# The beginning of the first attention layer: q and k projected step by step with the loading of the stream, their weights in halves on a second queue, the gate's projection last

## The chip, the cores and the metric

The kernel runs on one core of one Trainium2 chip. The metric is the device time of one execution in microseconds, as a median over runs. A profiled execution of the same program gives the trace: when each instruction ran on TensorE (PE, with its weight loads PEld), VectorE (DVE), ScalarE (ACT), GpSimd (POOL) and SyncE (SP), and what the DMA queues moved.

## The reference, cut to what matters

The program is a decoder trunk of two layers over 512 tokens of width 1024. The first layer is forgetting attention (FoX); the second, its MLPs and the latent attention are not touched by the change. What the changed part must compute:

```python
def fox_mixer(h, w_in, b_f, w_out):          # h = rms_norm(x, g)
    proj = h @ w_in                           # q, k, v: 1024 columns each; gate: 16
    q, k, v = ...                             # 16 heads of 64
    f_logit = proj[..., 3 * FOX_WIDTH:] + b_f
    cum = jnp.cumsum(jax.nn.log_sigmoid(f_logit), axis=1)
    # logits of a head: q.k * scale + cum[query] - cum[key], causal
    ctx = softmax(logits) @ v
    return ctx.reshape(B, S, FOX_WIDTH) @ w_out
```

## The kernel before, in words

Everything is float32 in two parts: a value is cast to a high part (ScalarE, `nc.scalar.copy`) and the difference is kept as a low part (VectorE). A product is then three matmuls, high by high, high by low and low by high (`three`, called by `linear`). The stream lies feature-major: eight tiles `xs[k]` of 128 features by 512 tokens. `scaled` multiplies a tile by the norm's gain and splits it into `h[k]`; the norm's factor per token (`rstd`) is applied later, to the results. Weights come in pieces, whose order stands in `pieces()` (L74) and, for the array in memory, in `_pack` (L1231). `piece(name)` takes the next one, and `emit_piece` (L202) loads it on SP's queue into one of two `raw` buffers and splits it into one of three `whi` and three `wlo` buffers, one piece ahead.

The FoX part begins at L433. SP is given x's eight tiles, with the gate's piece (16 columns of 8 steps, 64 KB) after the first and the first q piece (512 KB) after the fourth. Then come, as the program is written: `h`; the gate's projection into a bank `fps`, its weights spread into tiles of 128 columns a step that are cleared first, 24 matmuls; the squares of x and their sum; q's projection for the first pair of heads (24 matmuls); `rstd_of` (L276: eight small matmuls, then a reciprocal root on VectorE and GpSimd); k's (24); `rstd_tile` (L313: spread over 128 partitions by TensorE, copied by ScalarE); and v's first 512 columns in four pieces of 24 matmuls into four banks. After the first of these the program has `qk_parts` (L457), which scales and splits q and k, and `forget_sums` (L485): the gate's logits by rstd, bias, log-sigmoid, a cumulative sum of nine doubling steps on VectorE, and a store to `csc` in device memory. `start` (L540) loads a pair's two rows of it, broadcast over 128 partitions, into `nb`, and the softmax of each step subtracts that.

Attention runs in steps, one pair of heads and one block of 128 queries at a time, with two score banks. Between steps a `Filler` puts later matmuls: the next pairs' q and k projections, more of v, the output projection. Twelve are put ahead of the first step (L606), and 12 after each step.

No order is written by hand in this part. The instructions are ordered when the program is built, by the order in the text and by when each is expected to be ready, and each engine then works its own list in order. The engines' calls go through a wrapper, so nearly all rows of the trace carry its line, L111; they are told apart by their tiles (`acc`, `sc` and `tp` are the banks of this part, `r` the split tiles, `t` the plain ones).

Of the kernel before, what the change touches and what calls it, by code (L numbers as in the profile page):

```python
# [11 lines left out]
F32 = mybir.dt.float32  # L12
# [5 lines left out]
P = 128  # L18
D = 1024
S = 512  # L20
# [52 lines left out]

def pieces():  # L74

    out = [("f", 128)]
    out += [("qk", 1024)] * 2 + [("v", 1024)] * 4
    for p in range(1, FH // 2):
        out += [("v4", 1024)] * (2 * V4_BEFORE.count(p)) + [("qk", 1024)] * 2
    out += [("fo", 1024)] * 8  # L80
    out += [("ffn0", 1024)] * 40
    out += [("ka", 1024)] * 6
    out += [("kvb_v", 1024), ("kvb_n", 1024)] + [("qb_r", 384), ("qb_n", 768)] * 2
    out += [("kvb_n", 1024), ("qb_r", 384), ("qb_n", 768), ("kvb_v", 1024), ("qb_r", 384), ("qb_n", 768)]
    out += [("mo", 1024)] * 8
    out += [("ffn1", 1024)] * 32
    return out
# [9 lines left out]
def trunk(ctx: ExitStack, tc: tile.TileContext, xT, wts, gains, fing, rope, out):  # L97
# [53 lines left out]
    def nm(s):  # L151
        uid[0] += 1
        return f"{s}{uid[0]}"
# [7 lines left out]
    def tt(shape=(P, S)):  # L161
        return tp_.tile(list(shape), F32, tag="t", name=nm("t"))

    def f32(ap):
        return ap.bitcast(F32)
# [36 lines left out]
    def emit_piece(n):  # L202
        name, w = PIECES[n]
        raw = wpool.tile([P, 1024], F32, tag="raw", name=nm("raw"), bufs=2)
        nc.sync.dma_start(raw[:, :w], wts[OFFS[n] : OFFS[n] + P * w].rearrange("(p w) -> p w", p=P))
        if n in APART:

            his, los = [rt(), rt()], [rt(), rt()]
            for j in range(2):
                split(raw[:, j * S : (j + 1) * S], his[j], los[j])  # L210
            state["ready"][n] = [(his[k // 4][:, c], los[k // 4][:, c]) for k in range(KD) for c in [slice(k % 4 * P, k % 4 * P + P)]]
            return
        hi = wpool.tile([P, 1024], F32R, tag="whi", name=nm("whi"))
        lo = wpool.tile([P, 1024], F32R, tag="wlo", name=nm("wlo"))
        if name == "f":
            hv, lv = (t.rearrange("p (k c) -> p k c", c=P) for t in (hi, lo))
            rv = raw[:, :w].rearrange("p (k c) -> p k c", c=FH)
            nc.vector.memset(f32(hi), 0.0)
            nc.vector.memset(f32(lo), 0.0)
            nc.scalar.copy(hv[:, :, :FH], rv)  # L220
            nc.vector.tensor_tensor(lv[:, :, :FH], rv, f32(hv[:, :, :FH]), op=ALU.subtract)
        else:
            nc.scalar.copy(hi[:, :w], raw[:, :w])
            nc.vector.tensor_tensor(lo[:, :w], raw[:, :w], f32(hi[:, :w]), op=ALU.subtract)
        state["ready"][n] = (hi, lo)
# [35 lines left out]
    def scaled(x, gname, k):  # L261
        hi, lo = rt(), rt()
        nc.scalar.activation(out=hi, in_=x, func=AF.Copy, scale=g(gname, k))
        nc.vector.scalar_tensor_tensor(out=lo, in0=x, scalar=g(gname, k), in1=f32(hi), op0=ALU.mult, op1=ALU.subtract)
        return hi, lo
# [162 lines left out]
    with ExitStack() as fx:  # L428
        vpool = fx.enter_context(tc.tile_pool(name="fox_v", bufs=12))
        apool = fx.enter_context(tc.tile_pool(name="fox_a", bufs=2))  # L430
        dpool = fx.enter_context(tc.tile_pool(name="fox_d", bufs=1, space=bass.MemoryType.DRAM))

        xs = [tt() for _ in range(KD)]  # L433
        for k in range(KD):
            nc.sync.dma_start(xs[k], xT[:, k, :])
            if k == 0:
                emit_piece(0)
            if k == 3:
                emit_piece(1)
        h = [scaled(xs[k], "mix0", k) for k in range(KD)]  # L440


        fps = bank("acc")
        linear(fps, piece("f"), h)
        acc = xs[0]
        for k in range(KD):
            square_sum(acc, xs[k], k == 0, xs[k])
        qk = {}
        qk_ps = []
        for _ in range(2):  # L450
            qk_ps.append(bank("acc"))
            linear(qk_ps[-1], piece("qk"), h)
            if len(qk_ps) == 1:
                r = rstd_of(acc, D)
        rstd = rstd_tile(r)

        def qk_parts(pp, scale):  # L457
            t = tt()
# [25 lines left out]

        def forget_sums():  # L485

            z, e = tt(), tt()
            z, e = z[:FH], e[:FH]
            nc.vector.tensor_tensor(z, fps[:FH], rstd[:FH], op=ALU.mult)
            nc.vector.tensor_scalar_add(z, z, gsb[:FH, GCOL["bf"][0] : GCOL["bf"][0] + 1])  # L490
            nc.scalar.activation(out=e, in_=z, func=AF.Abs)
            nc.scalar.activation(out=e, in_=e, func=AF.Exp, scale=-1.0)
            nc.vector.tensor_scalar_add(e, e, 1.0)
            nc.scalar.activation(out=e, in_=e, func=AF.Ln)
            cur = tt()[:FH]
            nc.vector.scalar_tensor_tensor(out=cur, in0=z, scalar=0.0, in1=e, op0=ALU.min, op1=ALU.subtract)
            nc.vector.tensor_scalar_mul(cur, cur, -1.0)
            d = 1
            while d < S:
                nxt = tt()[:FH]  # L500
                nc.vector.tensor_copy(nxt[:, :d], cur[:, :d])
                nc.vector.tensor_tensor(nxt[:, d:], cur[:, d:], cur[:, : S - d], op=ALU.add)
                cur, d = nxt, 2 * d
            csc = dpool.tile([FH, S], F32, name="csc")
            nc.sync.dma_start(csc, cur)
            return csc

        accs = [bank(t) for t in ("sc", "sc", "tp", "tp")]
        for kp in range(4):
            whi, wlo = piece("v")  # L510
            for tb in range(NB):
                for k2 in range(2):
                    k = kp * 2 + k2
                    c = slice(k2 * S, (k2 + 1) * S)
                    t = slice(tb * P, (tb + 1) * P)
                    three(accs[tb], whi[:, c], wlo[:, c], h[k][0][:, t], h[k][1][:, t], k == 0, k == KD - 1, flip=True)
            if kp == 0:
                qk[0] = [qk_parts(pp, scale) for pp, scale in zip(qk_ps, QK_SCALES)]
                csc = forget_sums()
        for tb in range(NB):  # L520
# [710 lines left out]
def _pack(i):  # L1231
    W = FH * FHD
    parts = []
    fw = i["fox_w_in"][0]
    parts.append(_cols(fw, 3 * W, FH))
    parts += [_cols(fw, 0, P), _cols(fw, W, P)]
    b = _cols(fw, 2 * W, S)
    parts += [b[:, 2 * kp : 2 * kp + 2] for kp in range(4)]
    for p in range(1, 8):
        for q in range(2):  # L1240
            if V4_BEFORE[q] == p:
                b = _cols(fw, 2 * W + (q + 2) * 256, 256)
                parts += [b[:, :4], b[:, 4:]]
        parts += [_cols(fw, p * P, P), _cols(fw, W + p * P, P)]
    parts += [_cols(i["fox_w_out"][0], f * P, P) for f in range(8)]

    def up(layer):
        return [_cols(i["ffn_w_up"][layer], f * P, P) for f in range(DFF // P)]

    def down(layer):  # L1250

        w = i["ffn_w_down"][layer].reshape(DFF // HALF, 2, 2, P, 2, S)
        return [w[hf, :, a, :, b].transpose(1, 0, 2) for hf in range(DFF // HALF) for a in range(2) for b in range(2)]

    parts += up(0)
    parts += [_cols(i["ffn_w_down"][0][CHUNKS * D :], f * P, P) for f in range(8)]
    ka = i["mla_w_kv_a"]
    r = _cols(ka, KVR, ROPE)
    six = [_cols(ka, 0, P), _cols(ka, P, P), np.concatenate([r, r], axis=2)]
    six += [_cols(i["mla_w_q_a"][0], b * P, P) for b in range(3)]  # L1260
    for part in range(2):
        ks = list(range(4 * part, 4 * part + 4))
        parts += [np.concatenate([six[2 * n][:, ks], six[2 * n + 1][:, ks]], axis=1) for n in range(3)]
    kb = i["mla_w_kv_b"].reshape(KVR, MH, 2, NOPE)
    v = kb[:, :, 1].reshape(KVR, MH * NOPE)
    qb = i["mla_w_q_b"][0].reshape(QR, MH, NOPE + ROPE)
    vs = [_cols(v, half * S, S) for half in range(2)]
    ns = [np.concatenate([_blk(kb[:, h, 0], slice(None)) for h in range(4 * half, 4 * half + 4)], axis=1) for half in range(2)]
    qs = []
    for p in range(4):  # L1270
        qs.append(_blk(qb[:, 2 * p : 2 * p + 2, NOPE:].reshape(QR, 2 * ROPE), slice(None)))
        qs.append(np.concatenate([_blk(qb[:, 2 * p + e, :NOPE], slice(None)) for e in range(2)], axis=1))
    parts += [vs[0], ns[0]] + qs[:4] + [ns[1]] + qs[4:6] + [vs[1]] + qs[6:]
    parts += [_cols(i["mla_w_out"][0], f * P, P) for f in range(8)]
    parts += up(1)
    assert [x.size // P for x in parts] == [w for _, w in PIECES]
    parts += down(0)[: 2 * CHUNKS * 4] + down(1)
    return np.concatenate([np.ascontiguousarray(x).reshape(-1) for x in parts])
# [46 lines left out]
```

## Time and profile before

| | us |
|---|---|
| median of 3 runs | 1151.25 |
| lowest, highest | 1150.25, 1151.32 |
| the profiled execution's own time | 1152.35 |
| its span, first to last instruction | 1150.6 |

A profile is read from the engine that is busy for most of the span, and then from what ended its idle times. A row of the timeline gives the start in us, the duration in us, the engine, the line, the operation, the tile written and the tiles read, shapes and count; in brackets stands the idle time before it and what ended that. Where matmuls follow each other their rows overlap, because the duration includes the way through the array; their pace is read from their starts or from a chain's row divided by its count. A row of the chain of waits gives start, us, engine, tile and count.

### The profile page before, as it was taken

What the parts mean: (1) busy time and instruction counts of PE and PEld (TensorE: products, weight loads), DVE (VectorE), ACT (ScalarE), POOL (GpSimd) and SP (SyncE); (2) the same over time, 40 slices, a digit from 0 to 9 for tenths busy, and PEclk for the clock granted to TensorE, in tenths of its full rate; (3) what the DMA queues carried; (4) which work ended last, traced back from release to release, by engine and by line L of the source; (5) the groups of instructions that cost most, each with busy time, mean ns of one, the idle gap of its engine ahead of it and who ended that gap; (6) DMA issues with size and microseconds to landing.
All of it is one profiled execution on the core that took longest, in us unless ns stands there. A gap on an engine that the chain in (4) does not pass through costs nothing.

```text
span 1150.6 us, 14300 instructions
## 1 busy us (share of the span) xinstructions
PE 1122.5 (98%) x5356; PEld 916.1 (80%) x5356; DVE 783.1 (68%) x1413; ACT 574.6 (50%) x1053; POOL 24.0 (2%) x86
## 2 busy tenths in 40 slices
PE   8999999999999999999999899999999999999996
PEld 5777887787888888888887768788788888888875
DVE  6797888763457676677793688836356675765775
ACT  5555655553554454444352566635555544445611
POOL 1000000001000000000001100000100000000000
PEclk9999999999999999999999899999999999999998
DMA  5332222152815215212343121312531521611301
GB/s 186 130 102 81 75 82 84 37 165 85 317 37 167 90 55 183 74 56 65 119 159 105 34 65 51 110 55 92 187 143 58 185 68 56 201 56 37 128 1 74
DMA packets 36566, 116.66 MB, mean 101 GB/s; under 512 B 4224, under 2 KB 4864, under 8 KB 36496
## 3 DMA queue, kind: packets, MB, share of 16 engines
q1 hardware_dynamic: 35888, 114.15, 30.3%
q8 instruction: 42, 0.69, 0.2%
q0 software_dynamic: 320, 1.05, 0.2%
q10 hardware_dynamic: 288, 0.55, 0.1%
q14 instruction: 28, 0.23, 0.1%
HBM read 109.40 MB, written 6.32 MB: 101 GB/s over the span
## 4 chain that ended last, share of the span: by engine, by line
PE 92%; DVE 3%; DMA 2%; issue 1%; ACT 1%; POOL 1%; SPq 0%; POOLq 0%; ACTq 0%; DVEq 0%
PE up L111 33%; PE acc L111 20%; PE go L111 18%; PE sc L111 8%; PE tp L111 7%; PE keep L111 6%; DVE r L111 1%; DMA raw<-wts 1%; DVE wlo L111 1%; DVE t L111 1%; ACT r L111 1%; DMA t<-xT 0%; DMA nb<-csc 0%; DVE sl L111 0%; DVE rs L111 0%
## 5 line engine op out<-in xcount | busy, mean ns | idle before, releaser
L111 PE MATMUL acc<-r,whi 128*128 128x512 f32 x600 | 194.4, 404 | 5.0 <-ACT whi L111 5.0
L111 PE MATMUL up<-r,r 128*128 128x512 f32 x808 | 193.3, 391 | 2.5 <-DVE r L111 1.4
L111 PEld LDWEIGHTS up<-r,r 128*128 128x128 f32 x808 | 151.0, 188 | 34.9 <-DVE r L111 2.3
L111 PE MATMUL up<-r,whi 128*128 128x512 f32 x544 | 170.8, 390 | 0.8 <-ACT s L111 0.8
L111 DVE TENSOR_TENSOR t<-s,t 128x512 fp32r<-128x512 f32 x84 | 57.9, 689 | 127.5 <-ACT t L111 127.4
L111 DVE TENSOR_TENSOR wlo<-raw,whi 128x1024 fp32r<-128x1024 f32 (+3 forms) x95 | 111.3, 1171 | 39.4 <-ACT whi L111 38.8
L111 ACT CAST whi<-raw 128x1024 fp32r<-128x1024 f32 (+3 forms) x95 | 95.5, 1008 | 84.0 <-PE acc L111 33.5
L111 PEld LDWEIGHTS acc<-r,whi 128*128 128x128 f32 x600 | 109.6, 190 | 31.1 <-ACT whi L111 5.1
L111 ACT ACTIVATE s<-up 128x512 f32<-128x512 f32 x56 | 33.5, 597 | 190.8 <-PE up L111 190.8
L111 PEld LDWEIGHTS up<-r,whi 128*128 128x128 f32 x544 | 101.7, 188 | 22.4 <-ACT s L111 1.5
L111 PE MATMUL acc<-r,wlo 128*128 128x512 f32 x300 | 118.3, 394 | 0.1
L111 PE MATMUL up<-r,wlo 128*128 128x512 f32 x288 | 112.1, 389 | 0.0
L111 PE MATMUL go<-r,t 128*128 128x512 f32 x360 | 86.5, 389 | 0.0
L111 PE MATMUL sc<-r,r 128*128 128x512 f32 (+6 forms) x480 | 80.5, 356 | 1.6 <-ACT r L111 1.4
L111 PE MATMUL go<-whi,t 128*128 128x512 f32 x240 | 78.7, 389 | 0.0
L111 PEld LDWEIGHTS go<-r,t 128*128 128x128 f32 x360 | 67.6, 188 | 14.0
L111 PEld LDWEIGHTS sc<-r,r 64*128 64x128 f32 (+1 forms) x480 | 55.4, 186 | 25.0 <-issue 9.0
L111 ACT ACTIVATE t<-t,sm 128x512 f32<-128x512 f32 (+3 forms) x96 | 53.4, 558 | 34.7 <-DVE sm L111 34.2
L111 PEld LDWEIGHTS acc<-r,wlo 128*128 128x128 f32 x300 | 56.7, 189 | 12.9 <-DVE wlo L111 0.4
L111 DVE TENSOR_TENSOR r<-raw,r 128x512 fp32r<-128x512 f32 x72 | 46.5, 685 | 26.6 <-ACT r L111 26.6
L111 PEld LDWEIGHTS up<-r,wlo 128*128 128x128 f32 x288 | 54.1, 188 | 11.3
L111 DVE TENSOR_TENSOR r<-q,r 128x512 fp32r<-128x512 f32 x94 | 60.4, 684 | 0.0
(180 smaller groups left out, 1868.1 us busy)
## 6 DMA issues: line engine op xcount, KB each, us to landing
raw<-wts SPq DMA_DIRECT2D x122, 512.0 KB, 3.5
q<-wts SPq DMA_DIRECT2D x56, 512.0 KB, 4.6
nb<-csc SPq DMA_DIRECT2D x8, 512.0 KB, 4.7
t<-xT SPq DMA_DIRECT2D x8, 256.0 KB, 6.2
r<-xT SPq DMA_DIRECT2D x8, 256.0 KB, 6.0
xmid<-r SPq DMA_DIRECT2D x8, 256.0 KB, 6.9
r<-xmid SPq DMA_DIRECT2D x8, 256.0 KB, 4.2
xkeep<-r SPq DMA_DIRECT2D x8, 256.0 KB, 2.3
```

What stands on the lines that cost most here:

```text
L111: ins = fn(*args, **kw)
```

## The change

It touches the beginning of the FoX part, the gate's tiles and the order of the pieces.

- q's and k's first pieces come first in memory, then the gate, then v.
- Their `raw`, `whi` and `wlo` tiles are taken directly. Four loads, the halves of 512 columns (4 of the 8 contraction steps) of q and of k, are issued from ScalarE's queue; SP's queue has only x's eight tiles, back to back.
- One loop over the eight steps k: at k = 0 and k = 2 the halves are split, q's ahead of `scaled` and k's behind it (those of k = 2 serve steps 4 to 7); then three matmuls of that step for q and three for k, into two banks.
- The gate follows, through `piece("f")`. Its weights lie in one tile of 64 columns a step: high part in columns 0 to 15, low part in 32 to 47, zero between. Per step one matmul with 64 columns meets the high part of `h`, and one with the first 32 columns meets the low part: 16 matmuls. The two halves of the result (partitions 0 to 15 and 32 to 47) are added in `forget_sums`, by a copy on ScalarE across partitions and an addition on VectorE.
- Then the squares of x and `rstd_of`; `rstd_tile` comes after the first v piece.

```diff
 def pieces():
-    out = [("f", 128)]
-    out += [("qk", 1024)] * 2 + [("v", 1024)] * 4
+    out = [("qk", 1024)] * 2 + [("f", 128)] + [("v", 1024)] * 4
...
         hi = wpool.tile([P, 1024], F32R, tag="whi", name=nm("whi"))
-        lo = wpool.tile([P, 1024], F32R, tag="wlo", name=nm("wlo"))
+        lo = None if name == "f" else wpool.tile([P, 1024], F32R, tag="wlo", name=nm("wlo"))
         if name == "f":
-            hv, lv = (t.rearrange("p (k c) -> p k c", c=P) for t in (hi, lo))
+            hv = hi[:, : KD * 64].rearrange("p (k c) -> p k c", c=64)
             rv = raw[:, :w].rearrange("p (k c) -> p k c", c=FH)
-            nc.vector.memset(f32(hi), 0.0)
-            nc.vector.memset(f32(lo), 0.0)
+            nc.vector.memset(f32(hi[:, : KD * 64]), 0.0)
             nc.scalar.copy(hv[:, :, :FH], rv)
-            nc.vector.tensor_tensor(lv[:, :, :FH], rv, f32(hv[:, :, :FH]), op=ALU.subtract)
+            nc.vector.tensor_tensor(hv[:, :, 32 : 32 + FH], rv, f32(hv[:, :, :FH]), op=ALU.subtract)
+            hi = hv
...
         xs = [tt() for _ in range(KD)]
+        raws, his, los = ([wpool.tile([P, 1024], dt, tag=t, name=nm(t), **kw) for _ in range(2)] for t, dt, kw in (("raw", F32, {"bufs": 2}), ("whi", F32R, {}), ("wlo", F32R, {})))
+
+        def half(n, c):
+            c = slice(c * S, (c + 1) * S)
+            split(raws[n][:, c], his[n][:, c], los[n][:, c])
+
+        for c in range(2):
+            for n in range(2):
+                nc.scalar.dma_start(raws[n][:, c * S : (c + 1) * S], wts[OFFS[n] : OFFS[n] + P * 1024].rearrange("(p w) -> p w", p=P)[:, c * S : (c + 1) * S])
         for k in range(KD):
             nc.sync.dma_start(xs[k], xT[:, k, :])
-            if k == 0:
-                emit_piece(0)
-            if k == 3:
-                emit_piece(1)
-        h = [scaled(xs[k], "mix0", k) for k in range(KD)]
+        state["next"] = 2
+        h = []
+        qk = {}
+        qk_ps = [bank("acc"), bank("acc")]
+        for k in range(KD):
+            if k in (0, 2):
+                half(0, k // 2)
+            h.append(scaled(xs[k], "mix0", k))
+            if k in (0, 2):
+                half(1, k // 2)
+            for n in range(2):
+                c = slice(k * P, (k + 1) * P)
+                three(qk_ps[n], his[n][:, c], los[n][:, c], *h[k], k == 0, k == KD - 1)
 
         fps = bank("acc")
-        linear(fps, piece("f"), h)
+        fw, _ = piece("f")
+        for k in range(KD):
+            if k == KD - 1:
+                mm(fps[:32], fw[:, k, :32], h[k][1], start=False, stop=False)
+            mm(fps[:64], fw[:, k], h[k][0], start=k == 0, stop=k == KD - 1)
+            if k < KD - 1:
+                mm(fps[:32], fw[:, k, :32], h[k][1], start=False, stop=False)
         acc = xs[0]
         for k in range(KD):
             square_sum(acc, xs[k], k == 0, xs[k])
-        qk = {}
-        qk_ps = []
-        for _ in range(2):
-            qk_ps.append(bank("acc"))
-            linear(qk_ps[-1], piece("qk"), h)
-            if len(qk_ps) == 1:
-                r = rstd_of(acc, D)
-        rstd = rstd_tile(r)
+        r = rstd_of(acc, D)
...
         def forget_sums():
-            z, e = tt(), tt()
-            z, e = z[:FH], e[:FH]
-            nc.vector.tensor_tensor(z, fps[:FH], rstd[:FH], op=ALU.mult)
+            u, z, e = tt(), tt()[:FH], tt()[:FH]
+            nc.vector.tensor_tensor(u[:64], fps[:64], rstd[:64], op=ALU.mult)
+            nc.scalar.copy(z, u[32 : 32 + FH])
+            nc.vector.tensor_tensor(z, z, u[:FH], op=ALU.add)
...
             if kp == 0:
+                rstd = rstd_tile(r)
                 qk[0] = [qk_parts(pp, scale) for pp, scale in zip(qk_ps, QK_SCALES)]
                 csc = forget_sums()
```

In `_pack` the three first parts are put in the same new order.

More of the change, by code (lines that the diff above doesn't have):

```diff
@@ L1234, in _pack @@
     fw = i["fox_w_in"][0]
+    parts += [_cols(fw, 0, P), _cols(fw, W, P)]
     parts.append(_cols(fw, 3 * W, FH))
-    parts += [_cols(fw, 0, P), _cols(fw, W, P)]
     b = _cols(fw, 2 * W, S)
```

## The prediction

> **What bounds the kernel now.** I read the head of the page, then the busy time of TensorE in stretches, its timeline at the start, and the chain of waits.
>
> ```profile
> span 1150.6 us, 14300 instructions
> ...
> PE 1122.5 (98%) x5356; PEld 916.1 (80%) x5356; DVE 783.1 (68%) x1413; ACT 574.6 (50%) x1053; POOL 24.0 (2%) x86
> ```
>
> TensorE is busy for 98% of the span, so a microsecond counts only if it leaves TensorE's work or its idle time: 1150.6 - 1122.5 = 28.1 us in all.
>
> ```profile
> 0.00:4.99 4.99, 0.00 (x1) 1.00 0.47 134
> 4.99:12.22 7.23, 7.10 (x15) 1.00 0.97 334
> 12.22:27.48 15.26, 15.12 (x73) 1.00 0.45 148
> 27.48:49.34 21.86, 21.86 (x99) 1.00 0.32 101
> 50.00:250.00 200.00, 198.49 (x1147) 159.79 (x1146) 158.87 (x417) 116.81 (x275) 0.00 (x0) 1.00 0.27 89
> ```
>
> Columns: stretch, length, TensorE busy, clock, DMA share, GB/s (the last row has every engine; its DVE is 158.87). Nothing runs for 4.99 us. From 4.99 to 12.22 only 15 matmuls begin. Then TensorE is full: the end of the gate, q and k, then v, then attention with 1.51 us idle in 200.
>
> ```profile
> 4.99 1.39 PE L111 MATMUL acc<-r,whi 128*128 128x512 f32 x2 [4.99 <-ACT whi L111]
> ...
> 9.75 0.63 PE L111 MATMUL acc<-r,wlo 128*128 128x512 f32 x1
> ...
> 10.85 0.40 PE L111 MATMUL acc<-r,wlo 128*128 128x512 f32 x1
> ```
> ```profile
> 12.22 8.49 PE acc L111 x36
> 20.71 0.80 PE tp L111 x8
> ...
> 26.57 1.16 PE tp L111 x8
> ...
> 30.46 2.72 PE tp L111 x12
> ...
> 53.12 2.94 PE acc L111 x12
> 56.06 0.72 PE sc L111 x6
> ```
>
> The early rows are slow in a second way: a matmul takes 0.63 us up to 9.75 and 0.40 from 10.85, although the granted clock reads 1.00 in all stretches. Warm matmuls follow each other every 2.72 / 12 = 0.227 us; a slow one adds 0.23, so I estimate 0.45 from start to start. The slow phase lasts from 4.99 to some 10.3: 5.3 us.
>
> **The change, part by part.** *Fewer matmuls.* The gate took 3 products at 8 steps of the contraction, 24 matmuls of 512 columns. Packed side by side, high and low parts of its weights need 2, so 16. Eight by 0.227 is 1.82 us off a full TensorE.
>
> *The start.* Before, the first matmul needed x's first tile and 64 KB of gate weights. Now it needs x's first tile and half of the q weights, 256 KB each, with x's second tile on the way at the same time: 0.79 MB, and the 23 KB of gains, 0.81.
>
> ```profile
> 0.00:4.00 4.00, 0.00 (x0) 1.00 0.50 136
> 4.00:5.00 1.00, 0.01 (x1) 1.00 0.37 123
> 5.00:6.00 1.00, 1.00 (x2) 1.00 0.91 211
> 6.00:9.00 3.00, 3.00 (x6) 1.00 0.97 333
> 9.00:12.00 3.00, 3.00 (x9) 1.00 1.01 380
> ```
> ```profile
> 5.98 0.72 ACT L111 ACTIVATE r<-t,gsb 128x512 fp32r<-128x512 f32 x1 [1.04 <-DMA t<-xT]
> 6.60 0.61 ACT L111 ACTIVATE t<-t 128x512 f32<-128x512 f32 x1
> ...
> 9.88 1.03 ACT L111 CAST whi<-raw 128x1024 fp32r<-128x1024 f32 x1
> ...
> 29.18 1.22 ACT L111 CAST r<-t 128x512 fp32r<-128x512 f32 x2 [0.82 <-DVE t L111]
> ...
> 31.36 1.29 ACT L111 ACTIVATE t<-t 16x512 f32<-16x512 f32 x2 [0.96 <-DVE t L111]
> ```
>
> By 5.0 us 0.136 x 4 + 0.123 = 0.667 MB had moved; the missing 0.14 MB at 0.211 a microsecond lands at 5.7. The cast of a half is 1.22 / 2 = 0.61: first matmul at 6.4, or 7.1 if x's scaling (0.72) comes behind the cast on ScalarE. I take 6.6. All of x and both weights are 3.1 MB; 3.02 had moved by 12.0, so the last tile lands near 12.3. One step now feeds six matmuls, 1.36 us warm, against 0.72 on ScalarE for scaling, 0.31 for its share of the casts (2 x 0.61 - 1.03 = 0.19 more per piece than whole) and 0.61 for a square where one slips between (the row at 6.60 is a square, although the program has it after the gate). So once begun TensorE has a backlog. With 5.3 us slow at 0.45 it has begun 11.8 of its 64 matmuls by 11.9, and the other 52.2 end at 11.9 + 52.2 x 0.227 = 23.75. Before, 57 of the 72 were left at 12.22: 12.22 + 57 x 0.227 = 25.16. The start with the eight matmuls is worth 1.4 us: 1.82 less 0.4, since the later beginning eats almost what the backlog returns. Bounds: first matmul at 5.6 (the transfers at 0.380 a microsecond from 4.0 on) or at 8.0: 1.0 us better or 1.4 worse.
>
> The Trainium skill, "TensorE: Matmul & The Clock Gate", Part 1, says that the array runs at half speed until about 3.4 us of sustained activity. With 3.4 for 5.3 it would be 23.75 - 1.0 us; the 5.3 of the trace holds waits, so this speaks for a little more.
>
> *The reciprocal root.* The eight small matmuls of the sums of squares follow q and k and the gate, and spreading it over tokens follows the first v piece.
>
> ```profile
> 26.57 0.97 PEld L111 LDWEIGHTS tp<-ident,rs 128*128 128x128 f32 x8 [0.56 <-POOL rs L302]
> ```
> ```profile
> 27.76 0.59 ACT L111 COPY rstd<-tp 128x512 f32<-128x512 f32 x1 [0.48 <-PE tp L111]
> ```
>
> Before, the 24 k matmuls (5.45 us) all but covered the chain on VectorE and GpSimd, which began behind the sums (20.71 + 0.80 = 21.5) and ended at 26.5: 5.0 us. The v piece has 24 too, with three more v pieces behind it: I take 0.45 of the 0.56 us. Bounds 0 and 0.56.
>
> *The gate last.* The sums start at 23.75 instead of 20.71, so rstd, and with it q, k and the gate, come 3.05 us later. The gate's own chain grows by a copy across partitions (1.29 / 2 = 0.64 from the 16-row row above) and an addition, 0.67 below, with hand-overs 1.4.
>
> ```profile
> 29.66 0.67 DVE L111 TENSOR_TENSOR t<-acc,rstd 16x512 f32<-16x512 f32 x1
> ...
> 53.46 0.43 DVE L111 TENSOR_TENSOR nb<-nb,maskz 128x256 f32<-128x256 f32 x1 [0.45 <-DMA nb<-csc]
> ...
> 54.80 0.69 DVE L111 CUSTOM_DVE_ANT_0 t<-sc,nb 128x512 f32<-128x512 f32 x1
> ```
> ```profile
> 45.20 0.34 SPq L111 DMA_DIRECT2D csc<-t  x1
> ...
> 46.83 0.90 SPq L111 DMA_DIRECT2D nb<-csc  x2
> ```
>
> The chain runs from 29.66 to the store at 45.20, then two broadcasts at 46.83; VectorE waits for the second at 53.46, and the first softmax lets go of the score banks at 54.80 + 0.69 = 55.49. TensorE wants those banks for its second scores at 56.06: 0.57 us to spare. After, the banks come free at 55.49 + 3.05 + 1.4 = 59.94, and TensorE would be there at 56.06 - 1.85 = 54.2. The gap is 5.7 us. What covers it is the projection for the second pair of heads: 48 matmuls, of which the program puts 12 ahead of the first scores and 12 behind; the other 24 are 5.45 us, then comes the third pair. That later work is drawn forward is visible: q's first matmuls (they wait for the cast of 9.88) come before the gate's fifth step.
>
> ```profile
> 10.96 0.32 PEld L111 LDWEIGHTS acc<-r,whi 128*128 128x128 f32 x2 [0.15 <-ACT whi L111]
> 11.59 0.19 PEld L111 LDWEIGHTS acc<-r,whi 128*128 128x128 f32 x1 [0.31 <-ACT r L111]
> ```
> ```profile
> DVE nb L111 <- DMA nb<-csc: 9.8, 7, 3.1
> ...
> PEld sc L111 <- DVE sm L111: 1.6, 4, 0.5
> ```
>
> The cost lies between 0 and 5.7. Attention then has its filler early and must catch up while VectorE is 158.87 / 200 = 79% busy, enough to make up 5.7 us in some 30. But the order is fixed ahead, and the row on nb shows how well broadcasts are foreseen: VectorE waited for seven of them, 9.8 us, up to 3.1. TensorE's waits for the score banks were 0.5 at the longest. I take 0.6, near those. Queued behind the wait on VectorE are v's evacuations and the weights' low parts; on SP the store and the broadcasts have the weight loads behind them, each of which landed in time before.
>
> *At nothing:* the gate weights, loaded when a raw buffer is free, are needed only after 48 matmuls (10.9 us). The first v cast now waits for q's last matmul to free its buffer; 1.03 us of cast and the subtraction lie beside the gate's 16 matmuls (3.6 us). Without that cover: some 2 us. The two cleared tiles become one half as long, off the path.
>
> **Sum.** 1.82 - 0.4 + 0.45 - 0.6 = 1.25 us. The profiled execution took 1152.35, its span and 1.75 around it; it would become 1151.1. It lies 1.10 over the median of 1151.25, so on that footing 1150.0.
>
> **Rivals.** *A: two queues fill the slow start.* For it: at 4 to 5 us only 37% of the DMA engines' time is used, with several tiles issued. At 0.380 from 4.0 on, the 0.81 MB are in at 4.0 + (0.81 - 0.544) / 0.380 = 4.7 and the first matmul comes at 5.6, 1.0 us sooner; with that start and the gate covered in full (0.6) it is 1148.4. Against it: at 5 to 6 us the share is 91% at 211 GB/s, so sixteen engines were slow by themselves.
>
> *B: the second queue only takes turns from x.* If the weights' issue comes behind ScalarE's table load,
>
> ```profile
> 1.18 1.28 ACT L111 ACT_TABLE_LOAD   x1 [1.18 <-PEq L1318]
> ```
>
> it starts at 2.7 instead of 1.2, x is ahead, and equal shares bring the first half after 1.07 MB (6.6 us): first matmul at 7.6, the k half behind it some 0.4 late. That takes 1.4 us: 1151.4. The Trainium skill, "DMA: Bandwidth & Descriptors", section "Rules for kernel authors", says that issuing from several engines adds no bandwidth, as all share the same 16 DMA engines and interleave; by it A falls and this stands.
>
> *C: the gate is not covered.* If the next pair's weights or accumulator banks aren't there at 54 us, TensorE stands at the second scores for the whole 5.7 us. It decides from about 3 us of idle there; the price in full is 5.1 more than my term: 1155.1. Against it is TensorE's 1.51 us idle in 200 us of attention; for it, the broadcasts' waits.
>
> **How the numbers follow.** Forecast 1150.0: 0.42; A: 0.28; B: 0.15; C: 0.15. About 0.2% (2.3 us) is what a measurement of this kernel tells from no change: faster is below 1148.95, slower above 1153.55. Faster takes 0.24 of A and 0.08 of the forecast's lower end, 0.32; slower takes C, 0.15; same is 0.53. The range 1147.2 to 1153.6 leaves out most of C and A's lower end. The forecast's own, where the first matmul comes between 6.0 and 7.1 and the gate costs 0 to 2, is 1148.6 to 1151.4.
>
> **What would show it.** First matmul near 6.6; short matmuls from some 12; then no idle time until the sums, which begin near 23.8; no idle on TensorE for GpSimd; rstd near 30.8; the store near 49.7; TensorE busy with later projections from 54 to 60. Wrong: a first matmul before 5.5 or behind 7.5, x tiles waited for by ScalarE behind 10 us, or idle time over 2 us before scores between 50 and 80, or at the end of attention.

## The result, and the profile after

The change makes the kernel slower. The median is 1162.63 us (four runs, 1160.98 to 1166.22) beside 1151.14 us for the kernel before (four runs), a ratio of 1.0093 with a 95% interval of 1.0068 to 1.0118. The forecast was 1150.0 with a range up to 1153.6. The profiled execution of after took 1160.98 us, its span 1159.2; that is 8.6 us over the span of before. The other 2.9 us of the medians' difference lie between executions of the same kernel (last section).

The head of the page of after, then TensorE's busy time by stretch (stretch, length, busy time and matmul rows, granted clock, DMA share, GB/s):

```profile
span 1159.2 us, 14294 instructions
...
PE 1127.2 (97%) x5348; PEld 918.5 (79%) x5348; DVE 781.6 (67%) x1415; ACT 575.1 (50%) x1056; POOL 22.7 (2%) x86
```
```profile
7.35:18.12 10.77, 9.59 (x20) 1.00 0.60 210
...
65.65:69.06 3.41, 3.41 (x10) 0.50 0.00 0
50.00:250.00 200.00, 197.62 (x1121) 0.99 0.26 86
```

There are eight matmuls fewer (5348 for 5356), yet TensorE is busy 4.7 us longer: 1127.2 against 1122.5. Something made matmuls slower. Two stretches show it. From 7.35 to 18.12 only 20 matmul rows begin in 10.77 us. From 65.65 to 69.06 the granted clock is 0.50, where before has full clock. And 50 to 250 us has 200 - 197.62 = 2.38 us of idle time instead of 1.51, with 26 fewer matmuls begun.

To see where the time came from, I follow three places that both traces have. The first matmul is 2.36 us later (7.35 for 4.99). The last matmul of v's first columns is 2.48 us later (51.59 for 49.11). The 49th score matmul is 8.95 us later (99.53 for 90.58). From there to 182 us the two traces run in step, and at the end they are 8.6 apart (in between, at 672 us, 7.2; a stretch of half clock at 628 us stands in before only, one at 1103 us in after only). So there are two losses: **2.5 us at the start, and 6.5 us between the end of v and about 90 us.**

**The start.** ScalarE's timeline in after; the first row is its DMA queue:

```profile
4.73 1.28 ACTq L110 DMA_DIRECT2D raw<-wts  x2
6.06 0.62 ACT L110 CAST whi<-raw 128x512 fp32r<-128x512 f32 x1 [3.39 <-DMA raw<-wts]
6.58 0.72 ACT L110 ACTIVATE r<-t,gsb 128x512 fp32r<-128x512 f32 x1
8.04 0.62 ACT L110 CAST whi<-raw 128x512 fp32r<-128x512 f32 x1 [0.74 <-DMA raw<-wts]
10.53 0.62 ACT L110 CAST whi<-raw 128x512 fp32r<-128x512 f32 x1 [1.88 <-DMA raw<-wts]
11.06 0.72 ACT L110 ACTIVATE r<-t,gsb 128x512 fp32r<-128x512 f32 x1
```

ScalarE's list has the cast of q's second half (10.53) ahead of the scaling of x's second tile (11.06). That half serves steps 4 to 7; it lands at 10.51. x's second tile landed at 5.66 and its third at 7.79, and both stood behind a wait of 1.88 us for weights that nothing needed yet. TensorE's timeline shows what came of it:

```profile
7.35 0.79 PE L110 MATMUL acc<-r,whi 128*128 128x512 f32 x1 [7.35 <-ACT r L110]
8.70 1.22 PE L110 MATMUL acc<-r,whi 128*128 128x512 f32 x2 [0.56 <-ACT whi L110]
...
11.83 1.58 PE L110 MATMUL acc<-r,whi 128*128 128x512 f32 x2 [0.62 <-ACT r L110]
...
17.05 0.63 PE L110 MATMUL acc<-r,wlo 128*128 128x512 f32 x1
...
18.12 0.40 PE L110 MATMUL acc<-r,wlo 128*128 128x512 f32 x1
```

Two gaps of 0.56 and 0.62 us, and matmuls of 0.63 us up to 17.05 where before had 0.40 from 10.85. The trace's clock records give full clock from 17.9 us, 10.5 us after the first matmul; in before it is 10.6, 5.6 us after. In these records full clock is granted and taken away in steps of 3.413 us.

**The second scores.** The chain around the late gate. ScalarE copies rstd, SP's queue stores the gate's sums and loads them back:

```profile
35.72 0.58 ACT L110 COPY rstd<-tp 128x512 f32<-128x512 f32 x1
```
```profile
55.46 0.34 SPq L110 DMA_DIRECT2D csc<-t  x1
...
57.42 2.11 SPq L110 DMA_DIRECT2D nb<-csc  x2
```

VectorE then waits for the broadcast and runs the softmax of the first scores, head by head:

```profile
62.62 0.43 DVE L110 TENSOR_TENSOR nb<-nb,maskz 128x256 f32<-128x256 f32 x1 [1.53 <-DMA nb<-csc]
63.08 0.69 DVE L110 CUSTOM_DVE_ANT_0 t<-sc,nb 128x512 f32<-128x512 f32 x1
...
63.69 0.69 DVE L110 CUSTOM_DVE_ANT_0 t<-sc,nb 128x512 f32<-128x512 f32 x1
```

TensorE in after, and below it the one row of before for the same six score matmuls:

```profile
54.63 1.35 PE L110 MATMUL sc<-r,r 64*128 64x512 f32 x6
...
62.20 0.39 PE L110 MATMUL acc<-r,whi 128*128 128x512 f32 x1
63.83 0.79 PE L110 MATMUL sc<-r,r 64*128 64x384 f32 x3 [1.24 <-DVE sm L110]
64.55 0.50 PE L110 MATMUL acc<-r,whi 128*128 128x512 f32 x1
64.98 0.79 PE L110 MATMUL sc<-r,r 64*128 64x384 f32 x3
65.69 0.79 PE L110 MATMUL acc<-r,wlo 128*128 128x512 f32 x1
```
```profile
55.99 0.79 PE L111 MATMUL sc<-r,r 64*128 64x384 f32 x6
56.71 0.73 PE L111 MATMUL acc<-r,whi 128*128 128x512 f32 x2
```

From 55.91 to 62.2 TensorE is busy with later projections, as forecast. Then its list has none left ahead of the scores, and it stands 1.24 us. From 65.65 on the clock is half for 3.41 us, which costs half of that, 1.7. Third, the matmuls of the two heads are torn apart. Each uses 64 rows of the array; the six of both heads took 56.71 - 55.99 = 0.72 us in before, and in after three take 64.55 - 63.83 = 0.72 and the other three 65.69 - 64.98 = 0.71, 1.43 in all. Each head's three go as its own bank is let go (first softmax 63.08, second 63.69). Over the first 192 score matmuls (each counted to the next matmul's start, or to its own end where TensorE then stood) their time goes from 22.35 to 25.21 us, 2.86 more, all of it up to 86 us. Idle 1.24, clock 1.7, heads apart 2.86: 5.8 of the 6.5 us. The other 0.7 I did not resolve.

### The profile page after: what moved, and what is told of

The parts are those of the page before. It is cut to its first block, busy times and chain, and to the rows that moved or that the text cites. A ratio compares the mean times of both kernels' runs of the same rounds, so it can differ in the third digit from the quotient of the medians.

```text
span 1159.2 us, 14294 instructions
## 1 busy us (share of the span) xinstructions
PE 1127.2 (97%) x5348; PEld 918.5 (79%) x5348; DVE 781.6 (67%) x1415; ACT 575.1 (50%) x1056; POOL 22.7 (2%) x86
## 3 DMA queue, kind: packets, MB, share of 16 engines
q0 software_dynamic: 320, 1.05, 0.2%
## 4 chain that ended last, share of the span: by engine, by line
PE 91%; DVE 3%; DMA 2%; issue 2%; ACT 1%; POOL 1%; POOLq 0%; SPq 0%; ACTq 0%; DVEq 0%
PE up L110 33%; PE acc L110 20%; PE go L110 18%; PE sc L110 8%; PE tp L110 7%; PE keep L110 6%; DMA raw<-wts 1%; DVE t L110 1%; DVE r L110 1%; DVE wlo L110 1%; ACT r L110 0%; DMA nb<-csc 0%; DVE sl L110 0%; ACT whi L110 0%; DMA gsb<-gains 0%
## 5 line engine op out<-in xcount | busy, mean ns | idle before, releaser
L110 PE MATMUL acc<-r,whi 128*128 128x512 f32 (+1 forms) x600 | 195.7, 407 | 8.5 <-ACT r L110 8.0
L110 ACT CAST whi<-raw 128x1024 fp32r<-128x1024 f32 (+4 forms) x97 | 95.8, 991 | 98.0 <-PE acc L110 35.6
L110 PEld LDWEIGHTS acc<-r,whi 128*128 128x128 f32 (+1 forms) x600 | 110.5, 191 | 35.2 <-ACT r L110 9.0
L110 PE MATMUL sc<-r,r 128*128 128x512 f32 (+6 forms) x480 | 83.7, 357 | 2.5 <-DVE sm L110 1.2
```

The costliest lines, as they stand in the source:

```text
L110: ins = fn(*args, **kw)
```

## The experiments

Two theories. **Held start:** ScalarE's list holds x's tiles behind weights, and the gaps keep TensorE at half clock. **Late gate:** the gate's chain ends behind the work that TensorE has to cover it. Rivals: the second queue itself is the cost; the torn pairs are a fault of the order on TensorE alone; packing the gate is what hurts; VectorE, and not the gate's place, is what is late.

All kernels and the readings that decide. "v's end" and "49th score" are the places above, against before's profile; "lost" is their difference. Ratios are taken round by round, with 95% intervals; the medians of before in the three groups that ran together were 1151.65, 1151.61 and 1153.78 (four, four and four kernels, in the order of the table from e_order on).

| kernel | median us (runs) | ratio to before | full clock from | idle before second scores | v's end | 49th score | lost |
|---|---|---|---|---|---|---|---|
| after | 1162.63 (4) | 1.0093 [1.0068, 1.0118] | 17.9 | 1.24 | +2.48 | +8.95 | 6.5 |
| e_order | 1156.33 (10) | 1.0033 [1.0015, 1.0050] | 9.8 | 1.93 | -2.75 | +4.46 | 7.2 |
| e_one_queue | 1158.08 (6) | 1.0046 [1.0025, 1.0067] | 12.1 | 1.03 | -2.14 | +2.64 | 4.8 |
| e_rstd_late | 1157.30 (10) | 1.0054 [1.0031, 1.0077] | 9.6 | 1.56 | +0.02 | +4.87 | 4.9 |
| e_short_gate | 1158.63 (5) | 1.0062 [1.0030, 1.0094] | 14.8 | none | +0.91 | +2.26 | 1.4 |
| e_early_gate | 1153.22 (12) | 1.0012 [0.9994, 1.0029] | 11.9 | none | -1.39 | +1.62 | 3.0 |
| e_early_gate_only | 1155.94 (10) | 1.0035 [1.0017, 1.0052] | 16.9 | none | +1.93 | +4.96 | 3.0 |
| e_pairs | 1162.25 (4) | 1.0103 [1.0066, 1.0139] | 18.9 | 2.04 | +3.24 | +11.46 | 8.2 |
| e_packed | 1153.30 (10) | 1.0011 [0.9994, 1.0029] | 14.0 | 0.17 | +1.05 | +2.18 | 1.1 |
| e_warm_after | 1163.47 (5) | 1.0076 [1.0046, 1.0105] | 7.4 | 2.54 | -0.62 | +8.65 | 9.3 |
| e_best | 1152.36 (12) | 0.9986 [0.9970, 1.0003] | 11.7 | none | -1.29 | -0.77 | 0.5 |
| e_warm_best | 1150.84 (12) | 0.9993 [0.9970, 1.0017] | 6.8 | 1.06 | -3.14 | -1.28 | 1.9 |
| e_best_one_queue | 1152.45 (12) | 0.9987 [0.9964, 1.0010] | 9.2 | none | -3.25 | -3.12 | 0.1 |

### After with the walk's order written out (e_order)

On ScalarE, VectorE and TensorE the walk keeps a written order, in which the second halves are cast behind x's fifth scaling (s is a scaling, h the cast of a half, m three matmuls; the digits are piece and half or step).

```diff
-        for k in range(KD):
-            if k in (0, 2):
-                half(0, k // 2)
-            h.append(scaled(xs[k], "mix0", k))
...
+        order["on"], order["only"] = True, ("scalar", "vector", "tensor")
+        for what in ("s0", "h00", "m00", "s1", "m01", "h10", "m10", "m11", "s2", "m02", "m12", "s3", "m03", "m13", "s4", "h01", "m04", "h11", "m14", "s5", "m05", "m15", "s6", "m06", "m16", "s7", "m07", "m17"):
...
```

> The changed kernel with one thing different: in the walk over the eight steps ScalarE, VectorE and TensorE are held to a written order, in which the casts of the second halves stand behind the scaling of x's fifth tile, not ahead of its second. Loads as in the changed kernel. Theory 'held start' (ScalarE waits for a second half with x's tiles queued behind it; the gaps that this leaves on TensorE keep its clock at half until 17.9 us): no gap on TensorE after its first matmuls of k at 8.6 us, full clock one window of 3.4 us earlier (near 14.5), v's first matmul at 27.4 instead of 28.98 or 1.6 earlier again with two windows; total 1159 to 1161. Rival 'second queue' (the late landings by themselves set the start): v's first matmul within 0.5 us of 28.98 and the total unchanged, 1162 to 1163.

TensorE's timeline in this kernel:

```profile
6.88 1.22 PE L110 MATMUL acc<-r,whi 128*128 128x512 f32 x2 [6.88 <-ACT whi L110]
...
59.26 0.80 PE L110 MATMUL sc<-r,r 64*128 64x384 f32 x3 [1.93 <-DVE sm L110]
```

No gap at the start, full clock from 9.8, v's end 5.2 us earlier than in after: the held start is shown, and was worth more than I expected. It does not rest on one execution: in the four traces with after's walk (after, e_short_gate, e_early_gate_only, e_pairs) full clock came 7.8 to 12.1 us after the first matmul, in the five with the written order and no matmuls ahead of it 2.9 to 6.8 us after. The late gate is untouched. rstd is copied at 30.49 and the store issued at 50.24, where the prediction had 30.8 and 49.7, and 7.2 us are lost all the same, again with half clock for 3.4 us behind the idle time and 2.97 us more for the scores.

### The same with all loads on one queue (e_one_queue)

```diff
-        for c in range(2):
-            for n in range(2):
-                nc.scalar.dma_start(raws[n][:, c * S : (c + 1) * S], wts[OFFS[n] : OFFS[n] + P * 1024].rearrange("(p w) -> p w", p=P)[:, c * S : (c + 1) * S])
...
+        for what in ("x0", "w00", "x1", "w10", "x2", "x3", "x4", "w01", "w11", "x5", "x6", "x7"):
...
+                nc.sync.dma_start(raws[n][:, c * S : (c + 1) * S], wts[OFFS[n] : OFFS[n] + P * 1024].rearrange("(p w) -> p w", p=P)[:, c * S : (c + 1) * S])
```

> As the run with the written order, with all loads on SP's queue in the order of need: x 0, q's first half, x 1, k's first half, x 2 to 4, both second halves, x 5 to 7. Theory 'held start': within 1 us of the run with the written order, since the landings matter little once nothing is queued behind a late one. Rival 'second queue': first matmul at 5.5 to 6.2 instead of 7.35 and v's first matmul another 1 to 2 us earlier than with the written order on two queues.

The first matmul comes at 5.36 instead of 6.88, since the first half lands at 4.51 instead of 5.44, ahead of x's second tile. But full clock comes 2.4 us later, and v's end is not earlier. x's last tile lands at 12.55 us; in e_order it is 12.51 and in after 12.45. The second queue brings no rate here. The total is 1.8 us above e_order's, where under 1 was expected, with overlapping intervals: the second queue is not the loss, and no gain of it is clear of the noise.

### Before with rstd spread behind the first v piece (e_rstd_late)

```diff
-        rstd = rstd_tile(r)
...
             if kp == 0:
+                rstd = rstd_tile(r)
```

> The kernel before with one line moved: rstd is spread over the partitions after the first v piece, as in the change. Theory 'late gate' (q, k and the gate's chain come later, TensorE stands at the second scores, loses its clock for a window and takes the score pairs apart): start unchanged, last v matmul at 49.1, but 4 to 6 us lost between 50 and 90 us: 1155 to 1157. Rival 'start alone' (the loss in attention is only carried over from the start): within 1 us of the kernel before, 1150 to 1152.

TensorE in this kernel, at the first and the second scores:

```profile
53.15 0.93 PE L111 MATMUL sc<-r,r 64*128 64x512 f32 x5 [0.48 <-DVE v L111]
...
61.53 0.78 PE L111 MATMUL sc<-r,r 64*128 64x384 f32 x3 [1.56 <-DVE sm L111]
...
62.66 0.78 PE L111 MATMUL sc<-r,r 64*128 64x384 f32 x3
```

One line moved in the kernel before, and it loses 4.9 us: the start is before's, v ends within 0.02 us, and the second scores are late, torn apart (2.2 us more for the scores) and preceded by idle time. The late gate is shown without the change's start; the scaling of q and k is late here too, and the next experiment parts the two. rstd is copied 5.5 us later than before (33.27 for 27.76), and the second scores come 5.54 us later.

### After without the cumulative sum's doubling steps (e_short_gate)

It leaves out the nine doubling steps, which shortens the gate's chain, and so also takes 5.5 us of work from VectorE (776.1 us busy for 781.6).

```diff
-            while d < S:
+            while d < 1:
```

> The changed kernel without the nine doubling steps of the gate's cumulative sum, which are left out of the computation: the store comes some 8 us earlier, near 47.5 us. Theory 'late gate': no idle time on TensorE before the second scores, clock full from 18 us on, score pairs together, and the lag against the kernel before at 90 us falls from 8.95 to 2.5 to 3.5 us: total 1156 to 1157. Rival 'start alone': the lag at 90 us stays near 9 and the total at 1162.

TensorE in this kernel:

```profile
53.06 0.97 PE L110 MATMUL sc<-r,r 64*128 64x512 f32 x6
...
56.90 0.79 PE L110 MATMUL sc<-r,r 64*128 64x384 f32 x6
```

The six are together again, there is no idle time and no half clock behind it, and 1.4 us are lost instead of 6.5. The median falls by only 4 us (five runs, 1153.28 to 1162.15), less than expected, so it is the trace that carries this verdict. In this execution, the fastest of the five, full clock came at 14.8, a step earlier than in after, with gaps of 0.68 and 0.60 us like after's. The freed VectorE is a second difference, which e_rstd_late does not have.

### The gate early, with and without the written order (e_early_gate, e_early_gate_only)

The squares and the sums of squares go into the middle of the gate's matmuls, rstd is spread after 18 of the first v piece's 24, and the gate's chain is put ahead of q's and k's scaling. First on top of e_order, then on after alone.

```diff
+            if k == 4:
+                r = rstd_of(acc, D)
...
+                if kp == 0 and tb == 2:
+                    rstd = rstd_tile(r)
             if kp == 0:
-                rstd = rstd_tile(r)
-                qk[0] = [qk_parts(pp, scale) for pp, scale in zip(qk_ps, QK_SCALES)]
                 csc = forget_sums()
+                qk[0] = [qk_parts(pp, scale) for pp, scale in zip(qk_ps, QK_SCALES)]
```

> The run with the written order of the walk, and the gate's results early: the squares and the sums are put into the middle of the gate's 16 matmuls, rstd is spread after 18 of the first v piece's 24, and the gate's chain is put ahead of the scaling of q and k. If both theories hold ('held start' and 'late gate'): v's last matmul at 46.4 us as with the written order alone, the store to device memory near 45 instead of 51 or later, at most 1 us idle before the second scores, score pairs mostly together, and a lag against the kernel before of -2 to -3 us at 90 us that stays: total 1148 to 1150. Rival (VectorE cannot give the gate's chain and the v evacuations this early, and something else of the beginning of attention takes the time): lag at 90 us between 0 and +3: 1151 to 1154.

> The changed kernel with the early gate results alone, its walk as it was. 'Late gate': the loss between v's last matmul and 90 us falls from 6.5 us to under 2, with v's last matmul where the changed kernel has it (50.0 to 51.6): total 1155 to 1157. Rival 'start alone': lag at 90 us stays near 9.

TensorE in e_early_gate:

```profile
50.77 0.96 PE L110 MATMUL sc<-r,r 64*128 64x512 f32 x3
52.18 0.93 PE L110 MATMUL sc<-r,r 64*128 64x512 f32 x3 [0.45 <-DVE v L110]
...
55.99 0.78 PE L110 MATMUL sc<-r,r 64*128 64x384 f32 x3
...
57.13 0.78 PE L110 MATMUL sc<-r,r 64*128 64x384 f32 x3
```

The idle time before the second scores is gone in both, and 3.0 us are lost instead of 7.2 and 6.5; for the first no loss had been expected, for the second under 2. But now the first scores are torn apart: VectorE, busy with the gate first, is late with q, k and v ([0.45 <-DVE v]). The scores take 2.2 us more than in before, which with the 0.45 is most of the 3.0. The rival on VectorE came out in its numbers (1153.22, the 49th score at +1.62): VectorE's list has work for both, and what is put first makes the other late.

### After with the scores held together on TensorE (e_pairs)

The score matmuls of both heads keep the order in which they are written.

```diff
+            order["on"], order["only"] = True, ("tensor",)
+            order["last"].clear()
...
+            order["on"] = False
```

> The changed kernel with the score matmuls of a pair of heads held in the written order, so that one head's three are not drawn ahead of the other's. Theory 'pairs taken apart cost time': the groups of 0.72 to 1.45 us return to 0.48 to 0.90, 2.5 us less, lag at 90 us 6 to 7 instead of 8.95, total 1159 to 1161. Rival (TensorE then stands for the second bank as long as it gained): lag at 90 us 8.5 to 9.5, total 1162 to 1163.

TensorE at the second scores:

```profile
65.36 0.44 PE L110 MATMUL sc<-r,r 64*128 64x384 f32 x1 [2.04 <-DVE sm L110]
...
66.39 1.08 PE L110 MATMUL sc<-r,r 64*128 64x384 f32 x5
```

Nothing is won: the order among the six is fixed, but filler still gets between them (in the first eight steps 15 groups of score matmuls, where after has 12 and before 8), the scores take 24.98 us and the wait is 2.04. So the pairs were not whole here, and what whole pairs by themselves would save is not shown. In e_short_gate and e_best, where the banks come in time, the first eight steps are whole (8 groups) with no order fixed; that speaks for the late banks as the cause of the torn pairs.

### Before with the packed gate alone (e_packed)

The gate stays first, its 24 matmuls become 16, as in the change's diff.

> The kernel before with the packed gate alone: still first, 16 matmuls for 24, and the copy and addition across partitions in the gate's chain. Theory (matmuls removed count once TensorE is full): v's first matmul 0.9 to 1.8 us earlier, of which the gate's chain, 1.4 us longer with 0.57 to spare, takes about 1 back at the second scores: 1150 to 1151.5. Rival: with two matmuls a step instead of three while x arrives, TensorE is too little busy for the clock, which stays at half one window longer: v's first matmul up to 1 us later and 1152 to 1153.

TensorE in this kernel:

```profile
5.71 1.12 PE L111 MATMUL acc<-r,whi 128*64 128x512 f32 x2 [5.71 <-DVE whi L111]
7.16 1.42 PE L111 MATMUL acc<-r,whi 128*64 128x512 f32 x2 [0.34 <-ACT r L111]
...
27.61 1.16 PE L111 MATMUL tp<-ident,rs 128*128 128x128 f32 x8 [0.92 <-POOL rs L303]
```

The eight matmuls bring nothing here, as the rival had it; v even ends 1.05 us later. Two matmuls a step wait for x, the clock is full only at 14.0, and TensorE's wait for GpSimd behind the shorter stretch grows from 0.14 (its rows stand in the next section) to 0.92 us.

### After with 14 matmuls of zeros ahead (e_warm_after)

```diff
+        zero = rt()
+        nc.vector.memset(f32(zero), 0.0)
+        for _ in range(14):
+            mm(qk_ps[0], zero[:, :P], zero, start=True, stop=True)
```

> The changed kernel with 14 matmuls of a tile of zeros ahead of the walk, from some 2 us on, which fill TensorE until the first real matmul. Theory 'clock held at half' (a part of the start's loss is TensorE's half clock, kept up by the gaps): full clock at the first real matmul or one window behind it, v's first matmul at 26 to 27.5 instead of 28.98, total 2 to 3 us less: 1159 to 1161. Rival (the data alone set the pace up to 18 us, or the clock falls back in the gaps): v's first matmul within 0.7 us of 28.98, total unchanged.

TensorE, with the matmuls of zeros in its first row:

```profile
1.49 6.19 PE L110 MATMUL acc<-r 128*128 128x512 f32 x14 [1.49 <-DVE r L110]
7.52 0.40 PE L110 MATMUL acc<-r,whi 128*128 128x512 f32 x1
...
51.53 1.36 PE L110 MATMUL sc<-r,r 64*128 64x512 f32 x6
...
62.00 1.32 PE L110 MATMUL sc<-r,r 64*128 64x384 f32 x3 [2.54 <-DVE sm L110]
```

The first useful matmul takes 0.40 us, and v's end is 3.1 us earlier with after's order of work unchanged and a gap of 1.69 us still in it: most of the start's loss is the clock. Then nearly the whole gain is lost around the second scores (2.54 us idle, half clock for 6.8 us), and the time is after's. The store and the first softmax in this kernel:

```profile
52.38 0.34 SPq L110 DMA_DIRECT2D csc<-t  x1
```
```profile
61.25 0.69 DVE L110 CUSTOM_DVE_ANT_0 t<-sc,nb 128x512 f32<-128x512 f32 x1
```

The gate's chain did come earlier with the start: the store by 3.1 us (52.38 for 55.46). But from the store's issue to the softmax it took 8.9 us instead of 7.6, so the softmax is only 1.8 us earlier (61.25 for 63.08), TensorE stands 1.3 us longer, and the second step of half clock takes another 1.7. At the 49th score 0.3 of the 3.1 us are left. In e_order the chain came 5.2 us earlier and 4.5 us were left there.

### Both mended (e_best, e_warm_best, e_best_one_queue)

On top of e_early_gate the reciprocal root runs on VectorE alone, rstd is spread after 6 v matmuls, and q and k are scaled between the log-sigmoid and the cumulative sum, where `forget_sums` now yields. Then that with the 14 matmuls of zeros, and that with all loads on SP.

```diff
-                r = rstd_of(acc, D)
+                r = rstd_of(acc, D, alone=True)
...
-                if kp == 0 and tb == 2:
+                if kp == 0 and tb == 0:
                     rstd = rstd_tile(r)
...
-                csc = forget_sums()
+                sums = forget_sums()
+                next(sums)
                 qk[0] = [qk_parts(pp, scale) for pp, scale in zip(qk_ps, QK_SCALES)]
+                csc = next(sums)
```

> The written order of the walk with the gate still earlier: the reciprocal root wholly on VectorE instead of GpSimd (the chain of 4.3 us there becomes some 2), rstd spread after 6 of the first v piece's matmuls, and q and k scaled between the logarithm and the cumulative sum. If 'held start' and 'late gate' are the whole loss: v's last matmul near 46.4 to 47.7, the store near 43, no idle time before the second scores, the score groups of the first steps in one, and the lag against the kernel before at 90 us within 0.7 of the lag at v's last matmul (-1.4 to -2.75): total 1149 to 1150.5. Rival (with TensorE earlier, VectorE's evacuations of v bind the first scores): 1 to 2 us lost at the first scores, 1150.5 to 1152.5.

> The same with the 14 matmuls of zeros ahead of the walk. 'Clock held at half': v's first matmul at 22 to 23.5 in every execution, so the spread of the runs shrinks too; but the gate's chain doesn't come earlier by as much, so that a part of it is lost at the first scores: total 1148 to 1150. Rival (clock falls back in the gaps or the data set the pace): equal to the same kernel without them within 0.7 us.

> The earlier gate and the written order, with all loads on SP's queue in the order of need. 'Second queue is not needed': within 1 us of the same kernel on two queues, first matmul near 5.4 instead of 6.9 to 7.4. Rival 'second queue helps': 1.5 us or more slower, with x's last tiles landing later than 12.5 us.

TensorE in e_best, then in e_best_one_queue:

```profile
50.86 0.97 PE L110 MATMUL sc<-r,r 64*128 64x512 f32 x6
...
54.70 0.79 PE L110 MATMUL sc<-r,r 64*128 64x384 f32 x6
```
```profile
5.46 1.22 PE L110 MATMUL acc<-r,whi 128*128 128x512 f32 x2 [5.46 <-ACT whi L110]
...
48.90 0.97 PE L110 MATMUL sc<-r,r 64*128 64x512 f32 x6
...
52.74 0.79 PE L110 MATMUL sc<-r,r 64*128 64x384 f32 x6
```

In e_best the second scores are whole and on time, 0.5 us is lost, and the ratio to before is 0.9986 where after's is 1.0093: the two theories together are the whole of the loss. e_warm_best has v's end another 1.85 us earlier, but TensorE stands 1.06 us at the second scores, and its runs spread more than e_best's (1147.79 to 1158.47 beside 1149.64 to 1154.73), not less as expected. The profiled execution of e_best_one_queue keeps its 3.25 us lead of the start up to 90 us and ends 4.8 us below before's span. Against before, none of the three is clear of 1 by its interval: the medians differ by less than the executions of one kernel do.

## Why the prediction was wrong

**"With 5.3 us slow".** This step failed. It carried the slow phase of before over as a fixed length. It lasted 10.5 us, because gaps kept TensorE at half clock. The first matmul was the 7.1 case of the text (behind x's scaling) and a little more, 7.35 for 6.6. The text's own leaning, to a slow phase shorter than 5.3, went the wrong way. The sum of what was missed at the start: 0.75 us later, gaps 1.18, and the other 4.0 of the 5.2 us by which the slow phase was longer, at half pace, 2.0: 3.9. The difference to be explained is 2.48 + 1.85 = 4.33; the other 0.4 stays open.

**"Once begun TensorE has a backlog".** This sentence stood under it and was false. It counted ScalarE's work per step but took its order from need, and e_order shows that the order is what was lost: 5.2 us of v's end. The trace of before had a warning in the prediction's own fence, a square slipped in at 6.60.

**"The gate last ... I take 0.6".** The second step that failed, and the larger: 6.5 us, above the upper bound of 5.7. The chain's times were late mostly from the start (rstd at 35.72 for 30.8), but in e_order they came as forecast and the cost was 7.2. The cover was forecast rightly: TensorE did draw the later projections forward. What was missing is that half clock came behind the idle time of 1.24 and 1.93 us (1.7 us) and that, with the banks late, the two heads' matmuls were torn apart (2.9). The bound of 5.7 was standing time only. Rival C named the place; its price of 5.1 more was for another mechanism, and its chance of 0.15 rested on waits of before, which say little about a chain moved by 5 us. The start's 4.33 and this step's 6.47 - 0.6 are the 10.2 us between the lag that was forecast, -1.25, and the 8.95 at the 49th score.

**"I take 0.45 of the 0.56 us".** The 0.56 in the prediction's row is idle time of the weight loads. TensorE's own rows in before:

```profile
26.04 0.39 PE L111 MATMUL acc<-r,wlo 128*128 128x512 f32 x1
26.57 1.16 PE L111 MATMUL tp<-ident,rs 128*128 128x128 f32 x8
```

It stood from 26.43 to 26.57, 0.14 us, or 0.3 if counted from start to start (26.57 - 26.04 - 0.227). So this term was at least 0.15 us too large; beside the other two it is small.

**What held.** The last x tile near 12.3 (12.45); the first half near 5.7 (5.86); no idle time on TensorE for GpSimd. Rival A fell: two queues moved no more. The Trainium skill, "DMA: Bandwidth & Descriptors", section "Rules for kernel authors", says that spreading loads over engines brings no bandwidth; the traces agree within their spread (x's last tile landed at 12.01 to 12.86 in the nine with two queues, at 12.55 and 13.08 in the two with the same loads on one). Rival B had the start's direction, but not its reason: ScalarE issued its first loads at 1.24, not behind the table load. The eight matmuls are gone as planned, but e_packed shows no gain from them at a start which waits for data.

## What to carry to other kernels

A chain that ends in a wait of the busy engine is not covered because there is filler: count the filler's microseconds up to that wait, and price the wait with what follows it (here half clock and pairs torn apart) as well as with the standing time. Where the order is made by a scheduler, an in-order engine's list around a new load is the first thing to read, since one early cast of late weights held everything behind it. And a better start counts only as far as the chain that ends the next wait moves with it: of 5.2 us at the end of v e_order kept 4.5, of 3.1 e_warm_after kept 0.3.

## What the runs showed of the hardware

- The clock goes in steps of 3.413 us: stretches of half clock last 3.41, 6.83 or 10.24 us. From half clock, gaps of 0.56 and 0.62 us in neighbouring steps went with half clock in the next (after), while a step of e_order that was idle for its first 0.53 us was followed by full clock; 14 matmuls of zeros from 1.49 on had it full at 7.4 and 6.8.
- From full clock, the idle time in a step does not decide alone. In these traces every step in which TensorE stood 1.91 us or more was followed by half clock, and 2.54 us in e_warm_after by two steps of it. So were steps with 1.24 (after) and 1.72 us (e_order, a wait of 1.93 less what lay in the step before). But 0.92, 1.03 and 1.06 us were not, nor 1.18 at 281.69 in before and at 291.43 in after, nor 1.82 of a wait of 1.98 at 1094.23 in before, nor 1.56 in e_rstd_late, which lies across a border between steps. What else counts stays open. The Trainium skill, "TensorE: Matmul & The Clock Gate", Part 1, has a free-running window of about 3.4 us, which agrees; its section "Why this matters for your kernels" asks for no gaps over some 3 us, and here 1.91 was too much every time and 1.24 once.
- The clock column of the stretches read 1.00 in the slow start of before and of after; the duration of a matmul (0.63 or 0.40) shows it, the column doesn't.
- Executions of one program differ with their clock. The 30 runs of before beside e_best go from 1148.10 us at a mean clock of 0.996 to 1160.01 at 0.989, and 0.007 of the span is 8 of these 11.9 us; after's slowest (1166.22) was at 0.989, its fastest (1160.98) at 0.992. So one profile can lie some microseconds from its median, and comparisons of a few microseconds need the landmarks of the trace.
- Some loads were issued only as an earlier one landed. In after eight were in flight by 3.31; the ninth was issued at 4.54 (x's first tile landed at 4.53), then 4.73 (the gains, 4.71), 5.68 (x's second tile, 5.66) and 7.81 (x's third tile, 7.79). A limit of eight in flight fits the first three but not the last, when seven had been in flight since 5.86. So q's second half was issued only at 4.73, on a queue with nothing else to do; what sets this wait is open.
